# Attention scores on TensorE: the low-by-high term on 64 rows of the array, two ranges of keys side by side

## The chip, the cores and the metric

The kernel runs on one core of a Trainium2 chip. The metric is the device time of one execution in microseconds (us). Before the change it is 3247.66 us, the median of three runs (3247.56, 3247.66 and 3256.63).

## The reference

Two layers of a hybrid backbone. Each runs three token mixers on the same normalised input of 1024 latent and 256 context tokens with 1024 channels, merges them by gates and projects the result. Here only the first mixer matters, differential attention: 4 heads, each with two softmax maps over 64 channels.

```python
def one(qi):
    s = jnp.einsum('bhmqd,bhmkd->bhmqk', qi, k).astype(jnp.float32) * scale
    p = jax.nn.softmax(s, axis=-1)
    w = p[:, :, 0] - lam * p[:, :, 1]
    return jnp.einsum('bhqk,bhkd->bhqd', w.astype(v.dtype), v)
```

Latent queries see all 1280 keys (latents, then context). In layer 0 the 256 context queries see the 256 context keys alone; the last layer has no context queries. All is in fp32.

## The kernel before, in words

TensorE multiplies fast in a reduced form of fp32 (`F32R`), so the kernel splits each fp32 operand into a high part, rounded to that form, and a low part, what rounding left. A dense product is then three products: high by high, high by low, low by high (`mm3`, lines 182 to 185).

A layer runs in phases: A (attention, with dense blocks of the other mixers as filling), B, merging, output. In phase A each head does the following.

`kvq` (line 376) computes keys, queries and values, each as a dense block of 128 channels over chunks of 512, 512 and 256 tokens. A block's result is in the PSUM tile `pd`. For keys and queries `rope` applies the rotation, and `stack` (line 384) splits: a map has 64 channels, so the high and the low part of map m fit on the 128 partitions of one tile, `K[m]` and `q[m]`. For m = 0 the high part is on partitions 0 to 63, for m = 1 on 64 to 127. `evac_q` then makes `w[m]`, which is `q[m]` with its halves swapped, by four DMAs (line 434).

`attn` (line 443) makes the scores. `score(c, o, t, m)` handles 128 queries of map m. Its result S is a PSUM tile of three banks of 512 columns, of which there is one buffer. For each range of keys (0 to 511, 512 to 1023, 1024 to 1279) two products of 128 contraction rows go into the bank (line 456): `q[m]` with `K[m]` gives high by high plus low by low, `w[m]` with `K[m]` gives low by high plus high by low. A full score thus has six products, a context score two. Then VectorE takes the maximum over S (line 460), ScalarE the exponential (line 463), which reads S last and frees it. After both maps they are combined on ScalarE and VectorE (lines 471, 472), transposed on TensorE (line 493) and multiplied with the values into O (lines 183 to 185).

The order on each engine is the order in which the code records it. `attn` is a generator, and `interleave` puts pieces of the dense blocks (`fill`) between its steps. Waits between engines are set from the tiles. Loads of weights (`wr`, line 85) run some blocks ahead and are issued on SP's queue, as are all other DMAs here.

TensorE has its weights loaded ahead of each product, by an instruction of its own (PEld in the profile). One product has up to 128 contraction rows and 128 weight columns; where an operand has at most 64 rows, the product takes half of the array's rows, the half on which the operand's partitions lie.

Three other lines of TensorE work are read below: 611, the second layer of the filter network, whose operands are 64 rows by 64 columns and which runs on two opposite corners of the array; 256, products with 2 rows and 128 columns; and 266, products with 2 columns.

Of the kernel before, what the change touches and what calls it, by code (L numbers as in the profile page):

```python
# [9 lines left out]
F32 = mybir.dt.float32  # L10
# [17 lines left out]
KT = D // 128  # L28
# [27 lines left out]
class Weights:  # L56
    """128-column blocks of weights in their order of use: loads and splits run ahead."""
# [13 lines left out]
    def again(self, i):  # L71
        """Whether use i is of the same block as the last but one use."""
        a, b = self.order[i - 2], self.order[i]
        return i > 1 and a[0] == b[0] == "out" and (a[1], a[3]) == (b[1], b[3])
# [65 lines left out]
def whole(x):  # L140
    """Block k of x [128, blocks, n], as pieces (columns, their source)."""
    return lambda k: [(slice(0, x.shape[2]), x[:, k, :])]
# [14 lines left out]
def beside(main, side):  # L157
    """main, with a step of side for every other step of it."""
    for i, w in enumerate(main):
        yield w  # L160
        if i % 2:
            next(side, None)
# [7 lines left out]
class Kernel:  # L170
# [16 lines left out]
    def rsqrt(self, out, x, t):  # L187
        """out = x ** -0.5 for x > 0, by Newton's steps from a guess of the exponent's bits."""
# [13 lines left out]
    def mean_rsqrt_steps(self, pool, psum, ss, n, width, tag="P"):  # L202
        """[128, n] of rsqrt(mean + eps), alike on every partition, from the [128, n] squares summed but
        for the sum over the partitions: the sums come as columns, the roots go out as rows."""
# [21 lines left out]
    def block(self, key, chunks, psum, evac, ahead=True):  # L226
        """One block of 128 output channels over the chunks of tokens; yields the weight of each step."""
# [19 lines left out]
    def ada(self, pool, psum):  # L247
        """Shift and scale of layer 0's modulation: rows of 256 channels, turned into columns."""
# [26 lines left out]
    def ada_rest(self, pool):  # L275
        """The other parts of the modulation, by sums over the free dimension."""
# [55 lines left out]
    def hnorm_steps(self, l, c, xt, r, pool, tag=None):  # L332
        """Normalised, modulated input of layer l for chunk c, split for the products."""
# [22 lines left out]
    def hmod(self, l, c, x):  # L356
        """As hnorm_steps, from the normalised input x [128, KT, n], in place."""
# [18 lines left out]
    def kvq(self, l, h, P, psum):  # L376
        nc, A = self.nc, self.A
        K = [P.tile([128, NTOK], F32R, name=f"K{m}", tag=f"K{m}") for m in range(2)]
        Vh = P.tile([128, NKEY, 128], F32R, name="Vh", tag="Vh")
# [22 lines left out]
        def evac_k(c, ps):  # L402
            t0, n = CHUNKS[c]
            stack(rope(c, ps), K[0][:, t0:t0 + n], K[1][:, t0:t0 + n])

# [20 lines left out]
        def evac_q(c, ps):  # L426
# [4 lines left out]
            stack(rope(c, ps), q[0][:, 0:n], q[1][:, 0:n])  # L431
            for m in range(2):
                for a in range(2):
                    nc.sync.dma_start(out=w[m][64 * a:64 * a + 64, 0:n].bitcast(F32),
                                      in_=q[m][64 - 64 * a:128 - 64 * a, 0:n].bitcast(F32))
# [5 lines left out]
        self.kv = (K, (Vh, Vl), Q, turn)  # L441

    def attn(self, l, h, P, psum):
        nc = self.nc
        K, (Vh, Vl), Q, turn = self.kv
# [3 lines left out]
        def score(c, o, t, m):  # L449
# [3 lines left out]
            for a in range(k0, k1, 512):  # L453
                b = min(a + 512, k1)
                for i, st in enumerate((q[m], w[m])):
                    nc.tensor.matmul(S[:, a - k0:b - k0], lhsT=st[:, o + 128 * t:o + 128 * t + 128],  # L456
                                     rhs=K[m][:, a:b], start=i == 0, stop=i == 1)
# [18 lines left out]
        def values(c, o):  # L476
# [28 lines left out]
            sq = P.tile([128, 256], F32, name="osq", tag="osq", bufs=1)  # L505
# [70 lines left out]
    # A sequence of 8 blocks of 128 is transformed at 2048 points: frequency p + 16 m comes from  # L576
    # A_p = sum_b u_b cos(pi p b / 8) and B_p = sum_b u_b sin(pi p b / 8), p = 0..8, through 128 x 128
    # matrices. Pair p holds (real | minus imaginary) of its 128 frequencies; p = 0 and p = 8 share one pair,
    # whose row 0 is (frequency 0 | frequency 1024), both real. Pairs 5, 6, 7 take -B_p and hold plus imaginary.
# [4 lines left out]
    def filter_hidden(self, l, P, psum):  # L584
        """Hidden features of the filters, [64, tokens], rounded over what rounding left; the context's apart."""
# [55 lines left out]
    def butterfly(self, U, P, ZW, pool_share):  # L641
        """U: [128, 10, w] with block b in slot SLOT[b]; yields a group's [(A, B), (A, B)]."""
# [52 lines left out]
    def transform(self, ps, p, pool, ra, rb, ia, ib):  # L695
        """Pair p into ps [128, 2, w]."""
# [9 lines left out]
    def back(self, ps, p, pool, y):  # L706
        """Pair p of products y [128, 2, 128] back to (A | B), [channels, 256]."""
# [4 lines left out]
    def fold(self, s):  # L712
        """The sums over a and b of s [128, a, b, 128], both 2, in its first block."""
# [3 lines left out]
    def norm_of(self, ss, out, psum, P):  # L717
        """out [128, 1] = (sum of the squares in ss [128, 128] over rows) ** -0.5 by column."""
# [7 lines left out]
    def fix_dc(self, kt, ka):  # L726
        """Row 0 of the pair 0: two real products instead of a complex one."""
# [5 lines left out]
    def filters(self, l, q, P, M, psum, ZW):  # L733
        """Transform of the filters of channels 128 q.. (sum | difference of the two directions), to DRAM."""
# [1002 lines left out]
```

## Time and profile before

| | |
|---|---|
| median of the runs | 3247.66 us |
| span of the profiled execution | 3238.8 us |
| the median less that span | 8.9 us |
| TensorE products (PE) busy | 3014.6 us, 93% |
| TensorE weight loads (PEld) busy | 2529.3 us, 78% |
| VectorE (DVE) busy | 1807.2 us, 56% |
| ScalarE (ACT) busy | 1219.6 us, 38% |
| GpSimd (POOL) busy | 958.5 us, 30% |

The span goes from the first to the last instruction of one profiled execution; the runs' times hold some microseconds around it. Busy is the share of the span in which an engine has at least one instruction under way. The scores are made from 311.3 to 895.6 us (layer 0) and from 1894.8 to 2414.3 us (layer 1). A line such as L456 is a line of the kernel's source.

### The profile page before, as it was taken

What the parts mean: (1) busy time and instruction counts of PE and PEld (TensorE: products, weight loads), DVE (VectorE), ACT (ScalarE), POOL (GpSimd) and SP (SyncE); (2) the same over time, 40 slices, a digit from 0 to 9 for tenths busy, and PEclk for the clock granted to TensorE, in tenths of its full rate; (3) what the DMA queues carried; (4) which work ended last, traced back from release to release, by engine and by line L of the source; (5) the groups of instructions that cost most, each with busy time, mean ns of one, the idle gap of its engine ahead of it and who ended that gap; (6) DMA issues with size and microseconds to landing.
All of it is one profiled execution on the core that took longest, in us unless ns stands there. A gap on an engine that the chain in (4) does not pass through costs nothing. (4 is left out here: it accounts for less than half of the span.)

```text
span 3238.8 us, 43600 instructions
## 1 busy us (share of the span) xinstructions
PE 3014.6 (93%) x16220; PEld 2529.3 (78%) x16220; DVE 1807.2 (56%) x3822; ACT 1219.6 (38%) x2015; POOL 958.5 (30%) x640
## 2 busy tenths in 40 slices
PE   8898999999989889999999899999998888899998
PEld 4687878788878777788877778888886767778878
DVE  6754767676875756202356745546456677432343
ACT  4322535353532423212344444545454233222231
POOL 1442020202023333212543322121214554321441
PEclk9899999999999999999999999999999999999999
DMA  6323222222356655413442421221214556542342
GB/s 240 111 85 107 76 72 77 78 76 77 109 187 200 196 162 184 142 40 99 130 159 86 156 64 49 66 60 60 62 61 156 188 178 192 169 156 80 112 134 79
DMA packets 234740, 381.62 MB, mean 118 GB/s; under 512 B 22622, under 2 KB 125406, under 8 KB 233248
## 3 DMA queue, kind: packets, MB, share of 16 engines
q1 hardware_dynamic: 234528, 378.83, 36.4%
q8 instruction: 128, 2.10, 0.3%
q14 instruction: 84, 0.69, 0.1%
HBM read 278.74 MB, written 90.57 MB: 114 GB/s over the span
## 5 line engine op out<-in xcount | busy, mean ns | idle before, releaser
L183 PE MATMUL pd<-hh,wh 128*128 128x512 f32 (+1 forms) x2784 | 1051.1, 378 | 11.0 <-DVE r L397 6.2
L185 PE MATMUL pd<-hh,wl 128*128 128x512 f32 (+1 forms) x2784 | 1037.4, 373 | 2.1 <-POOL wl L104 2.1
L184 PE MATMUL pd<-hl,wh 128*128 128x512 f32 (+1 forms) x2784 | 1038.1, 373 | 0.4 <-DVE hl L350 0.2
L104 POOL TENSOR_TENSOR wl<-wr,wh 128x1024 fp32r<-128x1024 f32 (+1 forms) x177 | 413.1, 2334 | 1416.3 <-ACT wh L103 1302.0
L183 PEld LDWEIGHTS pd<-hh,wh 128*128 128x128 f32 x2784 | 532.6, 191 | 93.0 <-DVE r L397 6.9
L185 PEld LDWEIGHTS pd<-hh,wl 128*128 128x128 f32 x2784 | 531.9, 191 | 87.0 <-POOL wl L104 2.5
L184 PEld LDWEIGHTS pd<-hl,wh 128*128 128x128 f32 x2784 | 532.6, 191 | 79.2 <-DVE hl L350 1.2
L103 ACT ACTIVATE wh<-wr 128x1024 fp32r<-128x1024 f32 (+1 forms) x204 | 194.9, 956 | 288.2 <-PE pd L184 135.4
L463 ACT ACTIVATE e<-S,sm 128x1280 f32<-128x1280 f32 (+1 forms) x144 | 177.7, 1234 | 203.9 <-DVE sm L461 184.8
L460 DVE TENSOR_REDUCE sm<-S 128x1 f32<-128x1280 f32 (+1 forms) x144 | 197.2, 1369 | 72.0 <-PE S L456 71.3
L183 PE MATMUL pb<-gh,wh 128*128 128x512 f32 (+1 forms) x480 | 178.4, 372 | 8.4 <-ACT gh L199 7.0
L185 PE MATMUL pb<-gh,wl 128*128 128x512 f32 (+1 forms) x480 | 178.3, 371 | 5.0 <-POOL wl L104 3.4
L184 PE MATMUL pb<-gl,wh 128*128 128x512 f32 (+1 forms) x480 | 178.5, 372 | 2.9 <-DVE gl L200 2.8
L456 PE MATMUL S<-K,q 128*128 128x512 f32 (+1 forms) x400 | 149.2, 373 | 13.9 <-ACT e L463 13.8
L293 DVE SCALAR_TENSOR_TENSOR at<-aw,acs 128x256 f32<-128x256 f32 x224 | 115.2, 538 | 47.3 <-DMA aw<-in_ada_wT 40.8
L456 PE MATMUL S<-K,w 128*128 128x512 f32 (+1 forms) x400 | 136.1, 354 | 0.0
L1178 DVE TENSOR_TENSOR acc<-pb,sel 128x512 f32<-128x512 f32 (+1 forms) x40 | 25.4, 637 | 189.7 <-PE pb L185 189.6
L200 DVE TENSOR_TENSOR pl<-T,ph 128x512 fp32r<-128x512 f32 x164 | 109.5, 686 | 33.2 <-ACT ph L199 31.6
L199 ACT ACTIVATE ph<-T 128x512 fp32r<-128x512 f32 x164 | 94.4, 596 | 73.7 <-PE T L493 73.6
L1182 POOL TENSOR_TENSOR acc<-acc,sel 128x512 f32<-128x512 f32 (+1 forms) x70 | 86.6, 1250 | 84.7 <-DVE sel L1180 84.6
L183 PEld LDWEIGHTS pb<-gh,wh 128*128 128x128 f32 x480 | 90.7, 189 | 26.8 <-ACT gh L199 8.6
L472 DVE SCALAR_TENSOR_TENSOR e<-e,sm,e 128x1280 f32<-128x1280 f32 (+1 forms) x72 | 104.7, 1455 | 10.5 <-ACT e L471 10.0
(405 smaller groups left out, 5228.0 us busy)
## 6 DMA issues: line engine op xcount, KB each, us to landing
wr<-in_w_in SPq DMA_DIRECT2D x136, 512.0 KB, 3.4
fm<-in_fmat SPq DMA_DIRECT2D x99, 192.0 KB, 3.1
fm<-in_imat SPq DMA_DIRECT2D x72, 256.0 KB, 3.0
aw<-in_ada_wT SPq DMA_DIRECT2D x128, 128.0 KB, 2.5
wr<-in_w_out SPq DMA_DIRECT2D x28, 512.0 KB, 3.4
zd<-zz SPq DMA_DIRECT2D x48, 256.0 KB, 2.0
z<-zd SPq DMA_DIRECT2D x24, 512.0 KB, 4.8
gd<-ev SPq DMA_DIRECT2D x48, 256.0 KB, 2.4
```

The lines of the kernel that those rows point to most:

```text
L103: nc.scalar.activation(out=hi[:, 0:k, :], in_=t[:, 0:k, :], func=AF.Copy)
L104: eng.tensor_tensor(out=lo[:, 0:k, :], in0=t[:, 0:k, :], in1=hi[:, 0:k, :].bitcast(F32), op=SUB)
L183: mm(out, lhsT=wh, rhs=xh, start=first, stop=False)
L184: mm(out, lhsT=wh, rhs=xl, start=False, stop=False)
L185: mm(out, lhsT=wl, rhs=xh, start=False, stop=last)
L199: nc.scalar.activation(out=hi, in_=src, func=AF.Copy)
L200: nc.vector.tensor_tensor(out=lo, in0=src, in1=hi.bitcast(F32), op=SUB)
L293: nc.vector.scalar_tensor_tensor(out=t, in0=w, scalar=1.0, in1=cs[:, j, :], op0=MUL, op1=MUL, accum_out=sums[:, b, j, i:i + 1])
L456: nc.tensor.matmul(S[:, a - k0:b - k0], lhsT=st[:, o + 128 * t:o + 128 * t + 128], rhs=K[m][:, a:b], start=i == 0, stop=i == 1)
L460: nc.vector.reduce_max(out=sm[:, 0:1], in_=S[:, 0:nk], axis=AX.X)
L463: nc.scalar.activation(out=e[:, 0:nk], in_=S[:, 0:nk], func=AF.Exp, bias=sm[:, 1:2], scale=0.125, accum_out=sm[:, 2:3])
L472: nc.vector.scalar_tensor_tensor(out=e0[:, 0:nk], in0=e0[:, 0:nk], scalar=s0[:, 3:4], in1=e[:, 0:nk], op0=MUL, op1=ADD)
```

## The change

Three things change in phase A; the rest of the diff drops comments and moves line numbers.

First, what is formed: `q[m]` now holds the high part of the query on both halves of the partitions, so that its product with `K[m]` (high and low part) gives high by high plus high by low. What is missing is low by high alone, with a contraction over 64 rows. Low by low is no longer formed.

Second, the order in a score: the three products with `q[m]` come first, then three with the query's low part on 64 rows. Keys 0 to 511 and 1024 to 1279 use the half on which the high part of K lies. Keys 512 to 1023 use the other half; for these `w[1]` holds the query's low part, and a new tile `Kx` the keys' high part, on the other half of the partitions. The two halves have different banks of S.

Third, the copies: `evac_q` copies with four DMAs as before, two of the high part and two of the low part; `evac_k` copies the second chunk of keys to `Kx` with two DMAs per head. `osq`, a tile of the head's norm, now takes buffers of the tag `r1` of the rotation.

```diff
@@ kvq
+        Kx = P.tile([128, 512], F32R, name="Kx", tag="Kx")
@@ evac_k
             stack(rope(c, ps), K[0][:, t0:t0 + n], K[1][:, t0:t0 + n])
+            if c == 1:
+                for m in range(2):
+                    nc.sync.dma_start(out=Kx[64 - 64 * m:128 - 64 * m, :].bitcast(F32),
+                                      in_=K[m][64 * m:64 * m + 64, t0:t0 + n].bitcast(F32))
@@ evac_q
-            stack(rope(c, ps), q[0][:, 0:n], q[1][:, 0:n])
+            src = rope(c, ps)
             for m in range(2):
-                for a in range(2):
-                    nc.sync.dma_start(out=w[m][64 * a:64 * a + 64, 0:n].bitcast(F32),
-                                      in_=q[m][64 - 64 * a:128 - 64 * a, 0:n].bitcast(F32))
+                r, x = slice(64 * m, 64 * m + 64), slice(64 - 64 * m, 128 - 64 * m)
+                nc.scalar.activation(out=q[m][r, :], in_=src[r, :], func=AF.Copy)
+                nc.vector.tensor_tensor(out=w[0][r, :], in0=src[r, :], in1=q[m][r, :].bitcast(F32), op=SUB)
+                nc.sync.dma_start(out=q[m][x, :].bitcast(F32), in_=q[m][r, :].bitcast(F32))
+                nc.sync.dma_start(out=w[1][x, :].bitcast(F32), in_=w[0][r, :].bitcast(F32))
@@ score
-            for a in range(k0, k1, 512):
-                b = min(a + 512, k1)
-                for i, st in enumerate((q[m], w[m])):
-                    nc.tensor.matmul(S[:, a - k0:b - k0], lhsT=st[:, o + 128 * t:o + 128 * t + 128],
-                                     rhs=K[m][:, a:b], start=i == 0, stop=i == 1)
+            cols = [(a, min(a + 512, k1)) for a in range(k0, k1, 512)]
+            ts = slice(o + 128 * t, o + 128 * t + 128)
+            for a, b in cols:
+                nc.tensor.matmul(S[:, a - k0:b - k0], lhsT=q[m][:, ts], rhs=K[m][:, a:b], start=True, stop=False)
+            for a, b in cols:
+                x = a == 512
+                r = slice(64 - 64 * m, 128 - 64 * m) if x else slice(64 * m, 64 * m + 64)
+                nc.tensor.matmul(S[:, a - k0:b - k0], lhsT=w[x][r, ts], rhs=Kx[r, :] if x else K[m][r, a:b],
+                                 start=False, stop=True)
@@ values
-            sq = P.tile([128, 256], F32, name="osq", tag="osq", bufs=1)
+            sq = P.tile([128, 512], F32, name="osq", tag="r1", bufs=2)[:, 0:256]
```

The order of TensorE's products at the first full score of layer 0, before. S is the scores' tile, K the keys, q and w the query operands, T the transposes of the values, pd a dense block of the filling.

```order
L413 MATMUL T<-ident,vc 128x128 x4
L456 MATMUL S<-K_2117,q_2253 128x512
L456 MATMUL S<-K_2117,w_2255 128x512
L456 MATMUL S<-K_2117,q_2253 128x512
L456 MATMUL S<-K_2117,w_2255 128x512
L456 MATMUL S<-K_2117,q_2253 128x256
L456 MATMUL S<-K_2117,w_2255 128x256
L183 MATMUL pd<-hh_404,wh 128x512
```

The same place in the changed kernel:

```order
L418 MATMUL T<-ident,vc 128x128 x4
L463 MATMUL S<-K_2117,q_2256 128x512 x2
L463 MATMUL S<-K_2117,q_2256 128x256
L467 MATMUL S<-K_2117,w_2258 128x512
L467 MATMUL S<-Kx,w_2259 128x512
L467 MATMUL S<-K_2117,w_2258 128x256
L183 MATMUL pd<-hh_404,wh 128x512
```

The number of products is the same, and what stands ahead and behind. The products with w are now together, the last three, and on 64 rows (the rows here show the result's shape, not the contraction's). The row with Kx is on the other half of the array.

TensorE at the first context score of layer 0, between dense products, before:

```order
L184 MATMUL pd<-hl_504,wh 128x512
L456 MATMUL S<-K_2117,q_2343 128x256
L456 MATMUL S<-K_2117,w_2345 128x256
L185 MATMUL pd<-hh_503,wl 128x512
L183 MATMUL pd<-hh_503,wh 128x512
```

and in the changed kernel:

```order
L184 MATMUL pd<-hl_504,wh 128x512
L463 MATMUL S<-K_2117,q_2346 128x256
L467 MATMUL S<-K_2117,w_2348 128x256
L185 MATMUL pd<-hh_503,wl 128x512
L183 MATMUL pd<-hh_503,wh 128x512
```

Nothing moves there; the one product with w is on 64 rows, with whole-array products on both sides.

SP's queue of DMAs while the queries of the first head are evacuated, before (wr is a block of weights, aw and acs belong to the modulation):

```order
L286 DMA acs<-csd 128x2x256
L290 DMA aw<-in_ada_wT 128x256 x2
L85 DMA wr<-in_w_in 128x1024
L434 DMA w_2255<-q_2253 64x512 x2
L434 DMA w_2256<-q_2254 64x512 x2
L290 DMA aw<-in_ada_wT 128x256
```

and in the changed kernel:

```order
L286 DMA acs<-csd 128x2x256
L290 DMA aw<-in_ada_wT 128x256 x2
L408 DMA Kx<-K_2117 64x512
L408 DMA Kx<-K_2118 64x512
L85 DMA wr<-in_w_in 128x1024
L441 DMA q_2256<-q_2256 64x512
L442 DMA w_2259<-w_2258 64x512
L441 DMA q_2257<-q_2257 64x512
L442 DMA w_2259<-w_2258 64x512
L290 DMA aw<-in_ada_wT 128x256
```

The two DMAs of Kx stand ahead of a load of weights. The four of the queries are in the same place; the first of each pair copies q, the second w.

## Rows read from the trace of the kernel before

**Rows 1.** The page, part 1: busy time, share of the span, instructions.

```profile
PE 3014.6 (93%) x16220; PEld 2529.3 (78%) x16220; DVE 1807.2 (56%) x3822; ACT 1219.6 (38%) x2015; POOL 958.5 (30%) x640
```

**Rows 2.** Windows: length, busy by engine (instructions), granted clock, DMA share, GB/s.

```profile
500.00:550.00 50.00, 46.57 (x279) 39.99 (x279) 40.33 (x118) 27.27 (x42) 3.45 (x2) 1.00 0.27 82
...
2050.00:2100.00 50.00, 50.00 (x279) 42.14 (x277) 31.58 (x58) 30.68 (x45) 8.35 (x3) 1.00 0.16 54
```

**Rows 3.** Groups by shape, line 456: count, busy us, mean ns, idle before.

```profile
L456 PE MATMUL S<-K,q 128*128 128x512 f32 x256 | 107.7, 421 | 13.8 <-ACT e L463 13.8
...
L456 PE MATMUL S<-K,w 128*128 128x512 f32 x256 | 101.1, 395 | 0.0
...
L456 PE MATMUL S<-K,q 128*128 128x256 f32 x144 | 41.5, 288 | 0.1
L456 PE MATMUL S<-K,w 128*128 128x256 f32 x144 | 40.7, 283 | 0.0
```

**Rows 4.** Tile S, its maximum: count, ns min/median/max, first and last start.

```profile
L460 DVE TENSOR_REDUCE sm<-S x144: 404/1491/1494, 318.3 to 2414.7; 128x1 f32<-128x1280 f32 x128, 128x1 f32<-128x256 f32 x16
```

**Rows 5.** Timeline, TensorE, a full score and transposes: start us, duration us, instruction.

```profile
509.48 0.39 PE L456 MATMUL S<-K,q 128*128 128x512 f32 x1
509.71 0.39 PE L456 MATMUL S<-K,w 128*128 128x512 f32 x1
...
510.40 0.28 PE L456 MATMUL S<-K,q 128*128 128x256 f32 x1
510.52 0.28 PE L456 MATMUL S<-K,w 128*128 128x256 f32 x1
510.64 0.28 PE L183 MATMUL O<-ph,Vh 128*128 128x256 f32 x1
...
511.67 0.28 PE L185 MATMUL O<-ph,Vl 128*128 128x256 f32 x1
511.79 0.60 PE L493 MATMUL T<-ident,e 128*128 128x128 f32 x4
512.14 0.36 PE L183 MATMUL O<-ph,Vh 128*128 128x256 f32 x1
512.34 0.28 PE L184 MATMUL O<-pl,Vh 128*128 128x256 f32 x1
```

**Rows 6.** Timeline, TensorE, products on 64 rows between whole-array ones.

```profile
2453.04 0.39 PE L184 MATMUL pd<-hl,wh 128*128 128x512 f32 x1
2453.36 1.08 PE L611 MATMUL fp<-hid,fw 64*64 64x512 f32 x4
2454.36 0.50 PE L185 MATMUL pd<-hh,wl 128*128 128x512 f32 x1
2454.70 0.39 PE L183 MATMUL pd<-hh,wh 128*128 128x512 f32 x1
```

**Rows 7.** Timeline, weight loads of the same stretch; in brackets the loader's idle time.

```profile
2453.35 0.19 PEld L611 LDWEIGHTS fp<-hid,fw 64*64 64x64 f32 x4 [0.35 <-ACT vn L1122]
2454.36 0.19 PEld L185 LDWEIGHTS pd<-hh,wl 128*128 128x128 f32 x1 [0.81 <-issue]
```

**Rows 8.** Timeline, TensorE, only what is under way from 2453.30 to 2453.40.

```profile
2453.36 0.65 PE L611 MATMUL fp<-hid,fw 64*64 64x512 f32 x2
```

**Rows 9.** Timeline, TensorE, products with 2 rows and 128 columns.

```profile
31.02 0.81 PE L266 MATMUL pa<-aw,sc 128*2 128x256 f32 x3
31.77 0.28 PE L256 MATMUL pa<-ident,arow 2*128 2x2 f32 x2
31.98 1.05 PE L209 MATMUL msq<-ones,ss 128*128 128x2 f32 x8
```

**Rows 10.** Tiles q and w: count, ns min/median/max, first and last start; DMA landing.

```profile
L386 ACT ACTIVATE q<-pd x4: 379/379/382, 299.5 to 777.2; 64x256 fp32r<-64x256 f32 x4
...
L456 PE MATMUL S<-K,w x400: 274/389/628, 311.7 to 2414.4; 128*128 128x256 f32 x86, 128*128 128x512 f32 x48
...
DMA to landing us min/median/max: 2.0/2.3/4.3
```

More of the change, by code (lines that the diff above doesn't have):

```diff
@@ L440, in kvq @@
         yield from self.block(("in", l, BLK_V + h), (0, 1, 2), psum, evac_v)
-        self.kv = (K, (Vh, Vl), Q, turn)
+        self.kv = (K, Kx, (Vh, Vl), Q, turn)
     def attn(self, l, h, P, psum):
         nc = self.nc
-        K, (Vh, Vl), Q, turn = self.kv
+        K, Kx, (Vh, Vl), Q, turn = self.kv
         work = [(c, o) for c in self.chunks(l) for o in range(0, CHUNKS[c][1], 256)]
```

## The prediction

> **What bounds the kernel now.** I read the page first: TensorE is busy 93% of the span [rows 1], so whatever lengthens or shortens its stream of products is a candidate for the end time. Then the stretches of the attention phases. In layer 1, TensorE is busy for all of the 50 us from 2050 to 2100, with the clock granted in full (1.00, the 2.4 GHz level); in layer 0, from 500 to 550, it is busy 46.57 of 50 [rows 2]. So a microsecond of TensorE time inside a score is a microsecond of the end in layer 1, and nearly so in layer 0. Third, the score products by shape: 256 of 512 columns and 144 of 256 columns with each of the two left operands q and w, 800 in all, and only 13.8 us in which TensorE stood idle before one, waiting for the exponential that frees the tile S [rows 3]. The maximum that reads S ran 144 times, 128 times over 1280 keys and 16 times over 256 [rows 4]: 128 full scores of six products and 16 context scores of two.
>
> Last, the timeline of one full score: products start at 509.48, 509.71 ... 510.40, 510.52, and what follows starts at 510.64 [rows 5]. So one score costs TensorE 1.16 us; a 512-column product holds it for 0.23 us and a 256-column one for 0.12 us, start to start. Shown durations (0.39, 0.28) are longer, since a product's end overlaps the next one's start by 0.39 - 0.23 = 0.16 us. That overlap is what I use below: where it shrinks, TensorE stood.
>
> **The change, part by part.** *The products.* Per full score the three q products stay (0.23 + 0.23 + 0.12 = 0.58 us). The three w products, 0.58 us as well, become three on half of the rows: keys 0 to 511 and 1024 to 1279 on one half, keys 512 to 1023 on the other. If the halves run side by side this takes what the fuller half takes: 0.23 + 0.12 = 0.35 us. Saved: 0.23 us x 128 = 29.4 us. A context score has one key range: its w product, on half of the rows, still takes 0.12 us and saves nothing.
>
> Do halves run side by side? The only 64-row products of the trace are the second layer of the filter network, in pairs on opposite corners of the array (64 rows by 64 columns, line 611). The four instructions of one such group take 1.08 us in all [rows 6]; a window of 0.1 us at its head holds two of them, both started, together 0.65 us [rows 8]. So the second pair adds 1.08 - 0.65 = 0.43 us, two at a time. The new halves share the columns, which no row shows, but they write to different banks of S. I take it that they do run together.
>
> *The change of shape.* Now each score has one step from whole-array products to half-row products, and one back. Rows of the same filter group show what such a step costs. In: the product of line 184 starts at 2453.04 and the first 64-row one at 2453.36 [rows 6], 0.32 us instead of 0.23; the overlap is 2453.43 - 2453.36 = 0.07 us instead of 0.16. TensorE stood 0.09 us. Out: the group ends at 2453.36 + 1.08 = 2454.44, the next product is shown from 2454.36: overlap 0.08 us, again 0.08 to 0.09 lost. And the weights: an instruction of its own, PEld, loads them ahead of each product. The load for that next product starts only at 2454.36, with the product, after 0.81 us in which the loader had nothing to do [rows 7]; the product lasts 0.50 us instead of 0.39 and its successor starts 0.34 us behind it instead of 0.23 [rows 6]. So 0.11 us of a 128-column load lie bare, which a run of equal shapes hides. On the way in the bare load was 1.00 - 2 x 0.43 - 0.08 = 0.06 us for 64 columns; the new halves load 128 columns, so I take the 0.11 us of the nearest row with that width, and keep 0.06 as the lower end.
>
> Is it the shape or the data type, since those rows are plain fp32 and the scores are not? The transposes answer it: four fp32 products in the whole-array shape between products of the scores' kind. They start at 511.79, 0.12 us behind the 256-column product ahead, as any other would; they end at 511.79 + 0.60 = 512.39, and the next two 256-column products end at 512.50 and 512.62, 0.11 and 0.12 later [rows 5]. Nothing stood. And is it the columns or the rows? The two products with 2 rows and all 128 columns at 31.77 overlap the one ahead by 31.83 - 31.77 = 0.06 us and the whole-array one behind by 32.05 - 31.98 = 0.07 us [rows 9]. So fewer rows alone suffice.
>
> The Trainium skill, "TensorEngine Tiling (Array Packing)", Key Properties, has the same against this change: switching the tiling mode, not just the tile, drains TensorE; it gives no time for it, and the trace agrees with 0.09 us each way.
>
> One step in and out: 2 x (0.09 + 0.11) = 0.40 us, with 0.30 as the lower end (both loads at 0.06). All 144 scores pay: 57.6 us. Sum on TensorE: 57.6 - 29.4 = +28.2 us, that is 1.16 to 1.33 us for a full score and 0.23 to 0.63 for a context one. About 1 us of it falls where TensorE waits in layer 0 anyway (7% idle in [rows 2]); I take +27.
>
> *What hangs behind S.* The maximum (1.49 us, [rows 4]) and then the exponential start when the last product ends, 0.2 us later in a score, and the next score waits for that exponential. Where TensorE is the later one, as in layer 1, this is inside the 27 us; where it waits for S, the in-step lengthens that loop by the same amount and the out-step hides in the wait. No further term.
>
> *Copies, DMAs, tiles.* In the query's evacuation two ScalarE copies and two VectorE subtractions on 64 rows stay two and two. Four DMAs per chunk stay four; q now also waits for one. The last query copy starts at 299.5 and the first w product runs at 311.7; the copies land 2.0 to 4.3 us after issue [rows 10]. The value block between hides them; without it each head would lose a landing, 8 x 2.3 = 18 us at worst. I take 0. Two DMAs per head for Kx come ahead of a weight load on SP's queue and wait there for the K copies; that load is for a block that is used after the query block, so again 0, and the same 18 us at worst if it were not. The sum of squares now shares the two buffers of the rotary products, whose readers are long done: 0. No removed work can gain more than the 29.4 us, because nothing else in the diff leaves out an instruction.
>
> *Against the clock on record.* The profiled span is 3238.8 us; the median of the runs is 3247.7, 8.9 more, which I carry over. 3238.8 + 27 + 8.9 = **3275 us**.
>
> **The rivals.**
> *No cost of the step (faster).* A half-row product might follow a whole-array one without any stand, since both keep all 128 columns and the halves' weights could go in while the other half works. Then only the saving is left: 3247.7 - 29.4 = 3218. For it: no row has 64 rows with 128 columns. Against it: every step between shapes that I read has the short overlap, the 2-row one included. It decides where a step costs under 29.4 / 288 = 0.10 us.
> The Trainium skill, "TensorE: Matmul & The Clock Gate", Part 3, would have it so: its span for packed row tiles is one product's duration and about 4 ns per further tile, with no charge for coming from the whole array; rows 6 bear it out inside a group, not at its edges.
>
> *Loads ahead, no change.* TensorE drains, but the weights are loaded meanwhile. Then a step costs 0.09: 288 x 0.09 = 25.9, less 29.4: -3.5 us, 3244. For it: in whole-array runs each load lies beside the product ahead. Against it: the loader's 0.81 us of idleness ahead of 2454.36.
>
> *The halves do not run side by side (the change does not do what it says).* Sharing the columns, the second half waits for the first: the w products take 0.58 us as before and only the steps are left: 57.6 us, 3305.
>
> **How the numbers follow.** Forecast 0.70, no cost of the step 0.10, loads ahead 0.11, no side by side 0.09. The forecast's own range: with loads at 0.06 it is 144 x 0.30 - 29.4 = +13.8 us (3261); if the third half-row product's load lies bare too, 128 x 0.11 = 14 us more (3290). Cutting off the 3218 and the 3305 cases leaves out 0.19, so the range is 3243 to 3291. A measurement of this kernel can tell about 0.3%, 9.7 us, from no change: faster (under 3238) 0.11, same 0.12, slower (over 3257) 0.77.
>
> **What would show it.** In the changed profile's timeline of a full score: q products 0.23, 0.23 apart, then the first half-row product 0.20 to 0.21 behind the 256-column one instead of 0.12, lasting 0.50; the second half's product within some 10 ns of the first; the third 0.34 behind; the next whole-array product 0.21 behind that and lasting 0.50; 1.33 us in all. The loader idle ahead of both steps. TensorE's busy time up by some 27 us, and the span with it. I am wrong if the first half-row product follows after 0.12 us at a duration of 0.39 (no cost), or if the second half's starts 0.2 us behind the first's (no side by side), or if the added time sits at the first score of a head (a late copy).

## The result, and the profile after

The changed kernel takes 3263.67 us (median of 6 runs, 3253.61 to 3271.59), the kernel before 3247.61 us (6 runs, 3236.76 to 3256.63). The ratio is 1.0063, with a 95% interval of 1.0041 to 1.0085: slower by 13 to 28 us (the two medians by themselves are 16.1 us apart, 0.5%, which lies inside that interval). The forecast was 3275 us, a range of 3243 to 3291, and 0.77 for slower.

The profiled execution has a span of 3251.8 us, 13.0 more than the one of before. The page's part 1 of the changed kernel answers to [rows 1]:

```profile
PE 3038.9 (93%) x16220; PEld 2515.6 (77%) x16220; DVE 1803.3 (55%) x3822; ACT 1218.3 (37%) x2015; POOL 957.8 (29%) x640
```

TensorE is busy 24.3 us longer with the same number of products; every other engine is busy a little less than before. The span grew by 13.0 us only, so the other 11.3 us lie where TensorE stood idle before. The stretches that answer to [rows 2], with the same columns:

```profile
500.00:550.00 50.00, 49.82 (x289) 39.79 (x288) 39.48 (x116) 29.28 (x45) 4.80 (x2) 1.00 0.26 82
2050.00:2100.00 50.00, 50.00 (x256) 39.05 (x257) 29.21 (x56) 27.97 (x41) 7.18 (x3) 1.00 0.18 61
```

The clock is granted in full in both. A full score of layer 1 in the changed kernel's timeline (start us, duration us, instruction), the place of [rows 5]:

```profile
2058.94 0.39 PE L183 MATMUL pd<-hh,wh 128*128 128x512 f32 x1
2059.17 0.73 PE L463 MATMUL S<-K,q 128*128 128x512 f32 x3
2059.83 0.49 PE L467 MATMUL S<-K,w 64*128 64x512 f32 x1
2059.84 0.49 PE L467 MATMUL S<-Kx,w 64*128 64x512 f32 x1
2060.17 0.28 PE L467 MATMUL S<-K,w 64*128 64x256 f32 x1
2060.38 0.50 PE L184 MATMUL pd<-hl,wh 128*128 128x512 f32 x1
2060.71 0.40 PE L185 MATMUL pd<-hh,wl 128*128 128x512 f32 x1
```

Read it by ends. The three q products end at 2059.90, the first half-row product starts at 2059.83: an overlap of 0.07 us, where neighbours of one shape overlap by 0.16. It lasts 0.49 instead of 0.39. The other half's product starts 0.01 behind it and ends with it: they run side by side. The third starts 0.34 behind the first, ends at 2060.45, and the next whole-array product starts at 2060.38, again 0.07 ahead of that end, and lasts 0.50. The next follows after 0.33 instead of 0.23. The weight loads of the same stretch:

```profile
2059.83 0.18 PEld L467 LDWEIGHTS S<-K,w 64*128 64x128 f32 x1 [0.25 <-issue]
2059.83 0.18 PEld L467 LDWEIGHTS S<-Kx,w 64*128 64x128 f32 x1
2059.94 0.19 PEld L467 LDWEIGHTS S<-K,w 64*128 64x128 f32 x1
2060.37 0.19 PEld L184 LDWEIGHTS pd<-hl,wh 128*128 128x128 f32 x1 [0.25 <-issue]
```

At both steps the loader stood idle for 0.25 us and began only with the product. Between them it did run ahead: the third half-row product's weights went in at 2059.94, while the first two were under way. The other scores show the same: at all 148 places where a half-row product follows a whole-array one, the two overlap by 0.069 to 0.071 us; the loader's idle time ahead of a step has a median of 0.25 us in either direction; and the second half's product starts 0.003 us behind the first (median of 124).

The products by shape, to be set against [rows 3] (count, busy us, mean ns, idle before):

```profile
L463 PE MATMUL S<-K,q 128*128 128x512 f32 x256 | 83.0, 405 | 9.2 <-ACT e L474 9.2
L467 PE MATMUL S<-K,w 64*128 64x512 f32 x128 | 63.5, 496 | 0.0
L467 PE MATMUL S<-Kx,w 64*128 64x512 f32 x128 | 63.5, 496 | 0.0
```

All 256 half-row products of 512 columns lie close to their mean of 0.496 us (0.490 to 0.502): each bears a bare load, and each pair shares one.

**Where the time went.** The order of all products other than the scores', and the place of each score among them, is the same in both kernels, so the same product can be compared. First and last score of each layer, before:

```profile
L456 PE MATMUL S<-K,q x208: 274/389/795, 311.4 to 895.6; 128*128 128x512 f32 x64, 128*128 128x256 f32 x40
...
L456 PE MATMUL S<-K,q x192: 274/389/501, 1894.8 to 2414.2; 128*128 128x512 f32 x128, 128*128 128x256 f32 x64
```

and in the changed kernel:

```profile
L463 PE MATMUL S<-K,q x208: 274/389/507, 313.1 to 902.9; 128*128 128x512 f32 x64, 128*128 128x256 f32 x40
...
L463 PE MATMUL S<-K,q x192: 276/389/498, 1904.1 to 2428.3; 128*128 128x512 f32 x128, 128*128 128x256 f32 x64
```

It is 1.7 us behind at the first score, 7.3 at the last of layer 0, 9.3 at the first of layer 1, 14.1 at the last, 13.0 at the end. Two phases of scores made it.

For the account I take the products of the trace in order of time and call lost what lies between the ends of two neighbours beyond what the later one takes in a run of its kind (0.229 us for 512 columns, 0.117 for 256, 0.109 for a transpose). The profile models the ends of products, so one small difference is not exact; only differences above 0.02 us are counted. The stretches reach beyond the scores, in the kernel before from about 270 to 960 us and from 1885 to 2455. The sums, in us, hold to about 1 us, depending on where a stretch is cut:

| lost time of TensorE | before | changed | whole_rows | half_first |
|---|---|---|---|---|
| layer 0's attention, all | 68.3 | 94.2 | 73.8 | 97.5 |
| of it at products of S | 21.5 | 29.1 | 19.6 | 43.6 |
| of it at dense products (pd) | 14.0 | 31.4 | 21.8 | 24.4 |
| of it at transposes (T) | 10.3 | 6.2 | 9.6 | 6.7 |
| layer 1's attention, all | 16.5 | 37.6 | 16.4 | 37.5 |
| layer 0: time at the lower clock | 17.1 | 23.9 | 27.3 | 34.1 |

Layer 0 lost 25.9 us more, layer 1 21.1 more, and each of their 64 full scores saved 0.23: 14.7 each. Net +11.2 and +6.4; the rest of the span, where nothing was changed, is 4 to 5 us shorter and reads as scatter.

The table's last row is TensorE's granted clock. In layer 0 it falls to its lower level (1.2 GHz) for some microseconds at a time; in the changed kernel six of seven such falls come right behind a wait of TensorE. One of them, with the window from 304 to 306 us (columns as in [rows 2]):

```profile
302.30 0.47 PE L183 MATMUL pd<-hh,wh 128*128 128x512 f32 x1 [2.08 <-DVE w L440]
304.44 0.63 PE L184 MATMUL pd<-hl,wh 128*128 128x512 f32 x1
304.87 0.63 PE L185 MATMUL pd<-hh,wl 128*128 128x512 f32 x1
```
```profile
304.00:306.00 2.00, 2.00 (x6) 1.60 (x5) 0.00 (x0) 0.00 (x0) 0.00 (x0) 0.50 0.86 299
```

A product of 512 columns takes 0.43 us there instead of 0.23, so by an estimate from these two numbers 0.46 of the time at the lower clock is lost: 7.9 us before, 11.1 in the changed kernel, 12.7 with whole rows, 15.8 with half rows first. The runs' times go the same way: the changed kernel's three runs with a mean clock of 0.972 or 0.973 took 3253.61 to 3262.89 us, the three with 0.970 took 3264.45 to 3271.59.

### The profile page after: what moved, and what is told of

Read it like the earlier page. It is cut to its first block, busy times and chain, and to the rows that moved or that the text cites. A ratio compares the mean times of both kernels' runs of the same rounds, so it can differ in the third digit from the quotient of the medians.

```text
span 3251.8 us, 43641 instructions
## 1 busy us (share of the span) xinstructions
PE 3038.9 (93%) x16220; PEld 2515.6 (77%) x16220; DVE 1803.3 (55%) x3822; ACT 1218.3 (37%) x2015; POOL 957.8 (29%) x640
## 5 line engine op out<-in xcount | busy, mean ns | idle before, releaser
L199 ACT ACTIVATE ph<-T 128x512 fp32r<-128x512 f32 x164 | 94.2, 595 | 79.3 <-PE T L504 75.9
L463 PE MATMUL S<-K,q 128*128 128x512 f32 (+1 forms) x400 | 102.5, 360 | 9.2 <-ACT e L474 9.2
L183 PEld LDWEIGHTS pb<-gh,wh 128*128 128x128 f32 x480 | 90.7, 189 | 25.9 <-ACT gh L199 7.8
L185 PEld LDWEIGHTS pb<-gh,wl 128*128 128x128 f32 x480 | 90.8, 189 | 23.3 <-POOL wl L104 5.4
```

The lines of the kernel that those rows point to most:

```text
L183: mm(out, lhsT=wh, rhs=xh, start=first, stop=False)
L185: mm(out, lhsT=wl, rhs=xh, start=False, stop=last)
L199: nc.scalar.activation(out=hi, in_=src, func=AF.Copy)
L463: nc.tensor.matmul(S[:, a - k0:b - k0], lhsT=q[m][:, ts], rhs=K[m][:, a:b], start=True, stop=False)
```

## The experiments

Ratios are against the kernel before, timed beside it on the same chip, with a 95% interval.

**Whole rows.** The changed kernel, the last three products on all rows.

```diff
-                x = a == 512
-                r = slice(64 - 64 * m, 128 - 64 * m) if x else slice(64 * m, 64 * m + 64)
-                nc.tensor.matmul(S[:, a - k0:b - k0], lhsT=w[x][r, ts], rhs=Kx[r, :] if x else K[m][r, a:b],
-                                 start=False, stop=True)
+                nc.tensor.matmul(S[:, a - k0:b - k0], lhsT=w[0][:, ts], rhs=K[m][:, a:b], start=False, stop=True)
```

Expected:

> The changed kernel with all its copies and its order (three products with the query's high part, then three with its low part), but the last three on all 128 rows: the other half of the weights is the other map's low part, which meets the keys' low part and adds a term of the size of low by low. No change of shape is left, no product runs beside another. Theory (the change of shape costs 0.20 us each way, 0.23 us are saved, and a part of the cost falls where TensorE waits for S): 1.16 us inside a full score again and nothing behind it, so the time of the kernel before, within 0.3%, and the idle time at the scores' first product back to that of before (about 22 us by ends of products, against 14 in the changed kernel). Rival (the copies of q and Kx, or the order, cost the 16 us): stays at +0.5%. Rival for the waits (the order q first, not the longer score, shortened them): they stay at 14 us.

Measured 1.0020 (1.0009 to 1.0031). Inside a score it is 0.93 us from the end of the first product to that of the last, behind it nothing; in layer 1 TensorE loses 16.4 us, against 16.5 before. So without the shape the scores cost what they did, and copies and order cost layer 1 nothing. Layer 0 lost 5.5 us more than before, at dense products, of which 4.0 are a wait for the evacuation of the context queries; neither theory had that. The lower clock adds 4.7 us by the estimate above, and other losses shrank: products at the full clock lost 49.9 us against 51.0 before. By the two ratios (timed apart), 0.43%, some 14 us, is left for the shape, and some 6.5 us (3 to 10) is something else. The waits for S are back, which the tile's list of what ended idle time shows (us, times; before, the changed kernel, whole_rows):

```profile
  ACT e L463: 43.4, 61
```
```profile
  ACT e L474: 26.1, 28
```
```profile
  ACT e L471: 37.8, 63
```

61 waits for the exponential before, 28 in the changed kernel, 63 with whole rows in the same order of products. It was the steps, not the order q first, that shortened them.

**Same half.** All three half-row products on one half.

```diff
-                x = a == 512
-                r = slice(64 - 64 * m, 128 - 64 * m) if x else slice(64 * m, 64 * m + 64)
-                nc.tensor.matmul(S[:, a - k0:b - k0], lhsT=w[x][r, ts], rhs=Kx[r, :] if x else K[m][r, a:b],
-                                 start=False, stop=True)
+                r = slice(64 * m, 64 * m + 64)
+                nc.tensor.matmul(S[:, a - k0:b - k0], lhsT=w[0][r, ts], rhs=K[m][r, a:b], start=False, stop=True)
```

Expected:

> The changed kernel with all three low-by-high products on one half of the rows, one behind the other (Kx is copied but not read). Theory: the step of shape stays, the saving goes: 0.23 us more in each of 128 full scores than in the changed kernel, 29 us less some 2 us of waits; about 3291 us, +1.3% to +1.4% on the kernel before. Rival (the two halves do not really run beside each other, the shown overlap is how the profile draws them): as the changed kernel, +0.6%.

Measured 1.0158 (1.0139 to 1.0177), a little above what was expected; the interval's lower end touches it. In its timeline:

```profile
2075.74 0.83 PE L463 MATMUL S<-K,q 128*128 128x512 f32 x3
2076.49 0.85 PE L466 MATMUL S<-K,w 64*128 64x512 f32 x3
2077.27 0.50 PE L183 MATMUL pd<-hh,wh 128*128 128x512 f32 x1
2077.61 0.40 PE L184 MATMUL pd<-hl,wh 128*128 128x512 f32 x1
```

The half-row part takes 2077.27 - 2076.49 = 0.78 us instead of 2060.38 - 2059.83 = 0.55. That is the 0.23 us, and 1.0158 less the changed kernel's 1.0063 (timed apart from it) makes 31 us of 3240, where 29 were expected. The halves do run side by side.

**One product behind each full score**, on half of the rows and, as a control, on all. Into columns of S that nobody reads:

```diff
+            if c != 2:
+                r = slice(64 * m, 64 * m + 64)
+                nc.tensor.matmul(S[:, 1280:1536], lhsT=q[m][r, o + 128 * t:o + 128 * t + 128], rhs=K[m][r, 0:256],
+                                 start=True, stop=True)
```

(in the control without `r`). Expected, half a row first:

> The kernel before, with one more product behind the six of each full score: 256 columns on 64 rows, into columns of S that nobody reads. Theory: 0.40 us for the step in and out and 0.12 for the product, 128 times: 66 us, less about 9 us of waits: +1.7% (3300 to 3315 us). Rival (the step costs nothing, the 16 us come from elsewhere): +15 us, +0.5%, as with whole rows.

> As the one with a half-row product behind each full score, with all 128 rows: the control. Theory: 0.12 us x 128 = 15 us, +0.4% to +0.5%, and a timeline without any step: each product 0.23 or 0.12 us behind the last, the product behind the score 0.39 long. The difference between the two is then the price of the shape alone: 128 x 0.40 = 51 us less waits. If this one costs as much as the other, it is not the shape but one more product in S that costs.

Measured 1.0183 (1.0164 to 1.0202) for the half-row product and 1.0075 (1.0054 to 1.0097) for the whole-row one. The first is as expected; the control is a miss, above its 0.4% to 0.5%. In both, the one product more also moved scores among the dense products (65 of 150 stretches of score products stand where they stood in the kernel before), so the ratios hold more than the product; between the two runs the order is the same. The end of a score in the one:

```profile
2076.90 0.28 PE L456 MATMUL S<-K,w 128*128 128x256 f32 x1
2077.11 0.38 PE L460 MATMUL S<-K,q 64*128 64x256 f32 x1
2077.41 0.50 PE L183 MATMUL pd<-hh,wh 128*128 128x512 f32 x1
2077.75 0.39 PE L184 MATMUL pd<-hl,wh 128*128 128x512 f32 x1
```

and in the other:

```profile
2062.47 0.27 PE L456 MATMUL S<-K,w 128*128 128x256 f32 x1
2062.59 0.28 PE L459 MATMUL S<-K,q 128*128 128x256 f32 x1
2062.70 0.40 PE L183 MATMUL pd<-hh,wh 128*128 128x512 f32 x1
2062.94 0.40 PE L184 MATMUL pd<-hl,wh 128*128 128x512 f32 x1
```

From the last w product to the second one behind the score, 0.85 us against 0.47: the shape alone costs 0.38 us. In time the pair differs by 35 us, not 51 (41.7 between the profiled spans), since again there are fewer waits for the exponential (37 against 65 in the tile's list of idle time, and 9 us less lost at the scores' first product).

**Two products ahead of, or behind, each full score.** A test of what hides in the waits, two whole-row products of 256 columns each, once ahead of the six, once issued behind the maximum.

```diff
+            for _ in range(0 if c == 2 else 2):
+                nc.tensor.matmul(S[:, 1280:1536], lhsT=q[m][:, o + 128 * t:o + 128 * t + 128], rhs=K[m][:, 0:256],
+                                 start=True, stop=True)
```

Expected, ahead first:

> The kernel before, with two whole-row products of 256 columns ahead of the six of each full score, into columns of S that nobody reads. The maximum waits for S, so they lie inside the loop from score to exponential to the next score. 2 x 0.12 x 128 = 30 us. Theory: nothing hides them, the waits at a score's first product stay as before (22 us by ends of products) or grow: +30 us or a little more, +0.9% to +1.1%. Rival (TensorE's spare time in layer 0 hides such work wherever it stands): +20 us or less.

> The same two products issued behind the maximum instead, outside that loop; they stand some ten products behind the score, and the first waits for the maximum, which is over by then. Theory (work behind a score fills the time in which TensorE would wait for the exponential): the waits at the scores' first product shrink from 22 to about 14 us, as in the changed kernel, so +20 to +23 us, 8 us less than with the two ahead. Rival (the shrinking in the changed kernel has another cause): waits as before, +30 us.

Ahead: 1.0096 (1.0080 to 1.0111), 31 us, a number in the expected range. Behind: 1.0133 (1.0118 to 1.0148), 43 us, a miss. The test doesn't answer its question. The scores stand at other places among the dense products (with the two ahead fewer than a third of the stretches of score products stayed; in the runs with the changed kernel's products all 150 stay), presumably because the edits give the framework's scheduler other costs. That also corrects what stands ahead of the prediction: the order on an engine is the scheduler's, not just the recorded one. And the products behind the maximum brought a wait for it of their own, 12.7 us in layer 0:

```profile
PE S L462 <- DVE sm L460: 12.7, 5, 4.5
```

**Half rows first.** The changed kernel with the low-by-high products ahead of the whole-row ones.

```diff
-            for a, b in cols:
-                nc.tensor.matmul(S[:, a - k0:b - k0], lhsT=q[m][:, ts], rhs=K[m][:, a:b], start=True, stop=False)
...
                 nc.tensor.matmul(S[:, a - k0:b - k0], lhsT=w[x][r, ts], rhs=Kx[r, :] if x else K[m][r, a:b],
-                                 start=False, stop=True)
+                                 start=True, stop=False)
+            for a, b in cols:
+                nc.tensor.matmul(S[:, a - k0:b - k0], lhsT=q[m][:, ts], rhs=K[m][:, a:b], start=False, stop=True)
```

Expected:

> The changed kernel with the three half-row products of a score ahead of the three whole-row ones; everything else, and the order of all other products, as it is. The step to half rows now falls at the score's first product, the step back inside the score, and nothing behind it. Theory (a step costs 0.20 us wherever it stands; at a score's first product it hides where TensorE waits for S anyway): no cost behind the score (0.00 instead of 0.198), inside the score 0.90 to 0.93 us again, some 0.2 us at the first product where there was no wait; the sum within 4 us of the changed kernel, ratio 1.005 to 1.007. Rival (only a step behind the score can fill a wait, since the maximum starts when the score ends): 9 us more than the changed kernel, 1.009.

Measured 1.0070 (1.0057 to 1.0083).

```profile
2058.48 0.50 PE L465 MATMUL S<-K,w 64*128 64x512 f32 x1
2058.48 0.49 PE L465 MATMUL S<-Kx,w 64*128 64x512 f32 x1
2058.82 0.28 PE L465 MATMUL S<-K,w 64*128 64x256 f32 x1
2059.02 0.86 PE L468 MATMUL S<-K,q 128*128 128x512 f32 x3
2059.72 0.40 PE L183 MATMUL pd<-hh,wh 128*128 128x512 f32 x1
2059.95 0.39 PE L184 MATMUL pd<-hl,wh 128*128 128x512 f32 x1
```

Nothing stands behind the score now (0.40 long, 0.23 to the next), and layer 1 loses 37.5 us, against 37.6 in the changed kernel: there a step costs the same wherever it stands, and either place hides the same share of it. Each of its 59 undivided scores loses 0.192 to 0.202 us at the first product, the step and no wait beside it. Layer 0 loses 3.3 us more than the changed kernel, no more than its longer time at the lower clock accounts for (4.7 by the estimate). The trace does not have the rival's 9 us; the times alone, 1.0070 and 1.0063, could not exclude them.

**The order of the subtractions**, in three forms. The changed kernel's evacuation takes copy, subtraction, copy, subtraction. The edit puts both copies first:

```diff
-                nc.scalar.activation(out=q[m][r, :], in_=src[r, :], func=AF.Copy)
-                nc.vector.tensor_tensor(out=w[0][r, :], in0=src[r, :], in1=q[m][r, :].bitcast(F32), op=SUB)
...
+            for m, (r, x) in enumerate(half):
+                nc.scalar.activation(out=q[m][r, :], in_=src[r, :], func=AF.Copy)
+            for m, (r, x) in enumerate(half):
+                nc.vector.tensor_tensor(out=w[0][r, :], in0=src[r, :], in1=q[m][r, :].bitcast(F32), op=SUB)
```

First with whole rows and without Kx and the second low copy; expected:

> All six products of a full score on whole rows, as in the run with whole rows, but without the copies that this doesn't need (Kx, and the low part's second copy), and with the query's two copies by ScalarE ahead of its two subtractions by VectorE, so that these two stand side by side again. A whole-row product with the low part also forms a term of the size of low by low. The run with whole rows came out 0.2% over the kernel before; its trace puts the excess into layer 0, where TensorE waits 4.0 us for a subtraction that is held up behind modulation work. Theory (that excess is the order of the subtractions and perhaps Kx on SP's queue): ratio 1.000, within 0.1%, and no idle time of TensorE at that subtraction. Rival (it is scatter between runs, or the products' order in a score): 1.002 again.

Measured 1.0034 (1.0019 to 1.0048), a miss: slower, not 1.000. Its layer 1 is as before, 16.6 us lost; its layer 0 lost 84.9, 32.1 of them at S. But here too scores moved (29 of the 150 stretches, all in layer 0), so this is another order. The clock was at the lower level for 41.0 us of layer 0, against 17.1 before, which by the estimate is 11 of the 16.6 us more that it lost; products at the full clock lost less than before (44.4 against 51.0). So the run shows no cost of the order itself, and does not answer what it was made for.

Then in the changed kernel, where no product moved; expected:

> The changed kernel with that one edit, the query's two copies ahead of the two subtractions; the score's half-row products stay. Theory: the 4.2 us in which TensorE waits for the subtraction in layer 0 go, so 4 us less than the changed kernel, ratio about 1.005 against the kernel before; the step of shape stays with 0.20 us behind each score. Rival: those waits only move to the next thing that is late (the dense block's next tile), 1.006 as before.

Measured 1.0064 (1.0049 to 1.0079). What TensorE waited for in layer 0's attention (us, times, longest), in the changed kernel:

```profile
PE S L463 <- ACT e L474: 9.2, 5, 3.0
PE mrb L218 <- DVE mn L195: 8.0, 4, 2.2
PE pd L183 <- DVE w L440: 4.2, 2, 2.1
```

and with the subtractions together:

```profile
PE S L465 <- ACT e L476: 13.2, 5, 4.3
PE mrb L218 <- DVE mn L195: 8.0, 4, 2.2
```

The wait is gone, and the next waits for the exponential grew by the same 4.0 us; layer 0 lost 94.0 us in all, against 94.2. The rival was right, though the next late thing was the exponential and not a dense block's tile: the wait moved. The ratios are too wide to show 4 us by themselves.

Last, with the split order, the context scores' second product on whole rows (`r = slice(0, 128)` where `c == 2`). Expected:

> The changed kernel with the query's two copies ahead of its two subtractions (as in the run with the split order) and with the 16 context scores' second product on whole rows, so that these 16 have no step of shape. Whole rows add a term of the size of low by low there. Theory: 16 x 0.39 = 6 us less than the run with the split order, on the path in part, since context scores stand where TensorE also waits: 3 to 6 us, ratio 1.0045 to 1.0055; the time behind a context score falls from 2.8 us in all to 0. Rival (these steps lie in waits altogether): 1.0064 as before.

Measured 1.0048 (1.0033 to 1.0063). In layer 0 it lost 89.0 us, 5.0 less than with the split order alone, of which dense products 4.4; 1.6 of the 5.0 are the lower clock by the estimate. The ratio is the expected one, but the two intervals overlap and the profiled spans are only 0.5 us apart (3249.6 and 3250.1), so the gain is not shown in time. No version here beats the kernel before: a score saves 0.23 us and pays 0.38 to 0.40, of which the waits hide a part only.

## Why the prediction was right, and where it was off

*The bound.* Right in the main: the other engines are less busy, and the end moved with TensorE. But the span was to grow with TensorE's busy time, and it grew by 13.0 us where that grew by 24.3.

*Side by side.* Right, though no row of before had two halves with the same columns: 0.01 us apart, and 0.23 us a score dearer when put on one half.

*The step.* Right in both parts. The overlap of 0.07 and the load of 0.11 us came out as read from the filter network's products [rows 6, 7]; the wider load of 128 columns was the right one to take, as the 0.496 us show. Two of the rows were less clean than they were read: in [rows 7] the loader's idle time ahead of the way in ended with ScalarE's vn, so it may have been a wait, and in [rows 9] the product ahead of the 2-row ones has 2 columns, so only the way out tells of rows alone. The changed kernel settles both, with the overlap of 0.07 us at each of its steps in and no other engine named. Behind a full score TensorE loses 0.198 us (median of 123), inside one it gains 0.04 (0.889 us from first to last end, 0.929 before): 0.158 us net, where the prediction had 0.165 to 0.17. For 128 full scores that is 20 us and for 16 context scores 6 more.

The Trainium skill, "TensorEngine Tiling (Array Packing)", Key Properties, says that changing the tiling mode drains TensorE; the traces agree, with 0.09 us, and add the bare load, which costs a little more than the drain. The span formula for packed tiles in the Trainium skill, "TensorE: Matmul & The Clock Gate", Part 3, adds about 4 ns per further tile and leaves out the way in and the way out: inside a group the trace agrees (0.003 us between starts), at the edges 0.38 to 0.40 us come on top.

*The term that was mis-sized* is "about 1 us of it falls where TensorE waits in layer 0 anyway". It was more like 13, worked out from the profiled executions. The passage on what hangs behind S had the mechanism, that the out-step hides in the wait for S, and then put it at "No further term". In layer 1, the steps of 64 scores make 64 x 0.39 = 25 us, and the trace shows 21.1 lost more; in layer 0, 80 x 0.39 + 4.2 = 35 and 25.9 (in which some 3 us are the lower clock, for which the sum had no term). I had read the idle time of TensorE's products, 13.8 us in [rows 3], and taken the busy share of 1.00 in layer 1 to mean that nothing waits. But a score's first product may be held without TensorE falling idle: its load waits for the exponential while the product ahead still runs, and then lies bare. One score before, at 2043.67:

```profile
2043.39 0.39 PE L183 MATMUL pd<-hh,wh 128*128 128x512 f32 x1
2043.67 0.50 PE L456 MATMUL S<-K,q 128*128 128x512 f32 x1
2044.01 0.40 PE L456 MATMUL S<-K,w 128*128 128x512 f32 x1
```

with the load

```profile
2043.67 0.19 PEld L456 LDWEIGHTS S<-K,q 128*128 128x128 f32 x1 [0.33 <-ACT e L463]
```

and the same score in the changed kernel:

```profile
2054.19 0.39 PE L183 MATMUL pd<-hh,wh 128*128 128x512 f32 x1
2054.42 0.74 PE L463 MATMUL S<-K,q 128*128 128x512 f32 x3
```

Before, the product started 0.28 us behind its neighbour and lasted 0.50: 0.16 us lost with no idle time shown. In the changed kernel it starts at 0.23 and nothing is lost, since TensorE comes there 0.2 us later in relation to the exponential. Of 59 scores of layer 1 whose six products stand together, 28 lost over 0.03 us before, 30 with whole rows, 1 in the changed kernel. At the scores' first products that makes 3.0 us less in layer 1 and 5.8 in layer 0, at the transposes 4.1 more in layer 0. That the steps do this, and not the order, two pairs show, each with the same order of products within the pair: changed against whole rows (1 against 30 of the 59), and the half-row product behind against the whole-row one (4 against 29). Half rows first agrees, with the same loss in layer 1. The clean test of it, work that is not a step, failed as told.

*Copies, DMAs, tiles: 0.* Not quite. The two subtractions were costed as two and two, but in the changed kernel modulation work stands between them in VectorE's queue, one piece of it 2.64 us long in the first head, and the dense block's PSUM tile came free that much later: 4.2 us of waits in two places. On the path it was worth nothing that could be seen, as the split order showed. Of Kx no cost is seen in layer 1. The 0.2% of the run with whole rows, some 6.5 us that the sum had at 0, lies in layer 0 in the profiled execution, and most of it there is time at the lower clock. Whether the copies bring that about, by the waits ahead of it, is not shown: the one run meant to tell had another order and lay longer at the lower clock still.

*Against the clock on record.* The 8.9 us between span and median were not what lies around the span; the changed kernel's profiled run is 3253.61 us with a span of 3251.8, 1.8 more. Most of the 8.9 was the spread between runs (3236.76 to 3256.63). It fell out of the difference, but not out of the predicted time: the median of before is the base, and it moved by 0.05 only.

*The rivals.* No cost of the step, and loads ahead, are refuted by the loader's idle 0.25 us at each step; no side by side by the run on one half.

## What to carry to other kernels

A visit to half of the array's rows costs the way in and the way out, here 0.38 to 0.40 us together, so count columns saved per visit, not rows left empty: it pays only where one visit saves more than that, by more products in the same shape. Price a new operation from whatever rows of the same kind the trace has, however small their share of the time. And before charging a cost in full on a busy engine, look for products that start late or last long without idle time ahead of them: those are waits, and added work falls into them first.

## What the runs showed of the hardware

Two products on different row halves and the same columns start 0.01 us apart and share one bare load time. The step between shapes costs the same 0.2 us each way with half rows behind a score, in it or ahead of it; the 0.09 us of standing and the 0.11 us of a bare 128-column load are the same as around plain fp32 products. A weight load that waits for another engine is not run ahead either: it costs the same 0.11 us, with TensorE shown as busy throughout. A wait of TensorE can cost more than its length: behind the idle 2.08 us before 302.30 the granted clock fell to 0.50, and products of 512 columns took 0.43 us instead of 0.23 until it rose again.
